# One of a product group's weight sums made in DRAM by the DMA, nine more such groups, and idle memory put to use

## The chip, the core and the metric

The kernel runs on one core of a Trainium2 chip. TensorE (PE) multiplies, VectorE (DVE) and ScalarE (ACT) do elementwise work, GpSimd (POOL) and SyncE (SP) here do little computing: SP issues the loads of the weights. The metric is the time of one execution in microseconds on the device; lower is better. Before the change the median of three runs is 1473.39 us (1472.85 to 1474.01).

## The reference

One decoder layer on 256 tokens of width 2048, in float32: a combined input projection, a state-space half and an attention half, an output projection, and an MLP with a squared ReLU.

```python
u = rmsnorm(h, norm_mix_pre)
z, xbc, dt, q, k, v = split(u @ w_in)              # 2048 -> 12320 columns
y_ssm = ssd(conv(xbc), dt) gated by z, grouped rmsnorm
y_att = mixture of three causal dilated windows over q, k, v (16 heads of 128)
h = h + rmsnorm(concat(y_ssm, y_att) @ w_out)      # 4096 -> 2048
ff = relu(rmsnorm(h) @ w_up)                       # 2048 -> 8192
h = h + rmsnorm((ff * ff) @ w_down)                # 8192 -> 2048
```

Nearly all the time is in four matrix products: by w_in, w_out, w_up and w_down.

## The kernel before

**A product in float32 precision.** TensorE's fast float32 type (fp32r) keeps fewer bits, so every operand is split into hi + lo: ScalarE rounds it into hi (L139), VectorE takes the remainder into lo (L140). A product is then three matmuls: hi by hi, hi by lo, lo by hi (`row_tile`, L256 to L264). Activations are split once and kept; weights come from DRAM as raw tiles, 256 rows of 512 columns (512 KB, two blocks of 128 rows: KB = 2), by SP (`fetch`, L144), are split into a pair of tiles from a ring of five (`parts`, BUFS = 5), and used once. There are four raw tiles (RAWS = 4). Where the memory of dead activations is free, `fetch_next` takes raw tiles from that too (`uc`, where "ua", "ub" and "uc" are parts of one activation).

**A seven-product group.** For one step k (two row blocks) a plain treatment of two neighbouring column blocks a and b, for both halves of the tokens, is 8 products, 24 matmuls. `seven` (L311) does it in 7 products, 21 matmuls, in the way of Strassen and Winograd: it needs sums of weight blocks (`e`, two of them, `t4`, and the sum of b's two blocks, in place in `raw_b`) and sums of activations (`sums_of_acts`, L293, made once per k and kept in idle memory). All weight sums are adds on VectorE (`add_in_line`, L223; the add itself is L225), and `e`, `raw_b` and `t4` are then split like weights. Seven products go to four extra PSUM banks (`more`) and three of the four result banks (`acc`); `combine_new` adds `more` up on VectorE into SBUF after the last group of a unit.

**A unit** (`unit`, L362) is one such pair of column blocks over all of K: for each k in a given order either a plain pair (two calls of `row_tiles`) or a group; then the last plain steps, first for block a, then for b, each with a function at its end (`at_end`) that takes the result out of PSUM. For w_up that function (`up_end`) adds the combined part, scales, squares, and puts a generator (`turned`) on a list (`waiting`); it later transposes the result on TensorE into the same PSUM bank (L1223) and splits it (sl or al on VectorE). `pump` runs one step of that list after each k and block; at the first group of a unit `drain` runs the rest. The next unit uses the old `acc` as its `more`, so its first group writes the banks that these transposes use.

**The stages** in order: projections for the state-space half and its scan (to about 372 us), queries, keys and two units for the values (V), w_out (two units), the first half of w_up's hidden columns (a block of features in another layout and three units), w_down over them (two units), the second half of w_up (four units) and of w_down (two). Groups per unit: V 4; w_out 3 and 6; up 3 each (`UP_SEVENS`); down 5, 5, 5, 6: 59 in all.

**What sets the order.** Engines run their own queues in order. A scheduler places instructions by priority and by data they need; weights' splits and sums have high priority and are kept in program order on ScalarE and VectorE (`in_line`). GpSimd's queue has pow for the norms (`rmix`, `rmlp`, `rff`) and, in the state-space half, small products. The tile "junk" has one buffer, the temporaries "r" two.

Of the kernel before, what the change touches and what calls it, by code (L numbers as in the profile page):

```python
# [39 lines left out]
KB = 2  # L40
MASKED = -1.0e30
# [10 lines left out]
UP_SEVENS = (2, 4, 5)  # L52
V_SEVENS = (1, 3, 5, 6)

# [20 lines left out]
def hymba_layer(ctx: ExitStack, tc: tile.TileContext, x, norm_mix_pre, w_in, conv_w, conv_b, dt_bias, a_log,  # L75
# [38 lines left out]
    cst = cp.tile([P, consts.shape[1]], F32, name="cst")  # L114
    ident = cst[:, 0:P]
    triu = cst[:, P:2 * P]
    two = cst[:, 2 * P:2 * P + 32]
    m0 = cst[:, 2 * P + 32:3 * P + 32]
    m1 = cst[:, 3 * P + 32:5 * P + 32]
# [24 lines left out]
    def fetch(src, k0, c0, step=KB, into=None):  # L144

        raw = wp.tile([P, KB, NB], F32, name="raw", bufs=RAWS) if into is None else into
        for j in range(0, KB, step):
            rs = slice((k0 + j) * P, (k0 + j + step) * P)
            nc.sync.dma_start(raw[:, j:j + step], src[rs, c0:c0 + NB].rearrange("(k p) n -> p k n", p=P))
        return raw  # L150


    def tmp():
        if "own" in room:
            room["own"].rotate(1)
            return room["own"][0]
        return hp.tile([P, NB], F32, name="r", bufs=2)
# [8 lines left out]
    def in_place_of_u():  # L166
        a, b = big.tile([P, SUMS, 2, S], F32R, name="ua"), big.tile([P, KB, 2, S], F32R, name="ub")
        room["sums"] = [a[:, k] for k in range(SUMS)] + [b[:, k] for k in range(KB)]
        room["raw"] = big.tile([P, NK - SUMS - KB, NB], F32, name="uc")
        room["turn"] = -RAWS  # L170
        room["acts"] = part
        sums_of.clear()

    def in_place_of_h(acts):

        a = hp.tile([P, 3 * KB, 2, S], F32R, name="ha")
        room["sums"] = [a[:, k] for k in range(3 * KB)]
        if acts is part:
            b = hp.tile([P, KB, 2, S], F32R, name="hb")
            room["sums"] += [b[:, k] for k in range(KB)]  # L180
            room["sums"] += [hp.tile([P, 2, S], F32R, name="wpost", bufs=2) for _ in range(2)]
        else:
            b = hp.tile([P, NT, NB], F32, name="hb")
            room["shared"] = [[b[:, t] for t in range(NT)],
                              [hp.tile([P, NB], F32, name="wpost", bufs=2) for _ in range(NT)]]
        room["raw"] = None
        room["acts"] = acts
        sums_of.clear()

    def fetch_next(src, k0, c0):  # L190

        if room["raw"] is None:
            return fetch(src, k0, c0)
        turn = room["turn"]
        room["turn"] += 1
        n = KB * (turn % (RAWS + (NK - SUMS) // KB - 1) - RAWS)
        return fetch(src, k0, c0, into=None if turn < 0 or n < 0 else room["raw"][:, n:n + KB])
# [3 lines left out]


# [20 lines left out]
    def add_in_line(dst, a, b):  # L223
        with in_line():
            line["dve"] = nc.vector.tensor_tensor(dst, a, b, op=ALU.add)  # L225
# [85 lines left out]
    def seven(src, ca, cb, k, acc, more, first, last):  # L311
# [4 lines left out]
        with tc.high_priority(offset=AHEAD):  # L316
            raw_a = fetch_next(src, k * KB, ca)
            raw_b = fetch_next(src, k * KB, cb)
            e, t4 = sum_tile(), tmp()
            add_in_line(e[:, 0], raw_a[:, 0], raw_b[:, 0])  # L320
            add_in_line(e[:, 1], e[:, 0], raw_b[:, 1])
# [3 lines left out]
            add_in_line(raw_b[:, 0], raw_b[:, 0], raw_b[:, 1])  # L325
# [33 lines left out]
    def order_of(ks, by_seven):  # L359
        return [(k, k in by_seven) for k in ks]  # L360

    def unit(src, n, order, last, acc, more, combine, lag=0, at_end=(None, None), first=True, ending=None):  # L362
# [17 lines left out]
        for b in range(2):  # L380
            if b and ending:
                ended.append(ending(cols[b], last, acc))
            else:
                row_tiles(src, cols[b], last, acc[b::2], room["acts"], False, True, lag if b else 0, at_end[b],
                          fetch=fetch if b else fetch_next)
# [41 lines left out]
    cw = cp.tile([P, 4, 32], F32, name="cw")  # L427
    bias_b = cp.tile([P, 32], F32, name="bias_b")
    a_b = cp.tile([P, 32], F32, name="a_b")
    skip_b = cp.tile([P, 32], F32, name="skip_b")  # L430
# [19 lines left out]
    def load_parameters():  # L450
# [4 lines left out]
        nc.sync.dma_start(cst[:, P:], consts[:, P:])  # L455
# [77 lines left out]
    with tc.high_priority(offset=2 * AHEAD), tc.manual_schedule():  # L533
        nc.sync.dma_start(cst[:, 0:P], consts[:, 0:P])
# [21 lines left out]
    rbq = cp.tile([P, S], F32, name="rbq")  # L556

    mid = ExitStack()
# [5 lines left out]
    dt = cp.tile([P, NT, 32], F32, name="dt")  # L564
    dA = cp.tile([P, NT, 32], F32, name="dA")
    acs = cp.tile([P, NT, 32], F32, name="acs")
    eacs = cp.tile([P, 32], F32, name="eacs")
    toend = cp.tile([P, 32], F32, name="toend")
# [240 lines left out]
    def in_place_of_last_heads():  # L809
# [3 lines left out]
        room["raw"], room["acts"] = None, act_u  # L813
# [5 lines left out]
    def two_values(vb):  # L819
# [16 lines left out]
        unit(w_in[:, COL_V:], vb, order_of(range(7), V_SEVENS), (7,), acc, more,  # L836
# [15 lines left out]
    waiting.append(in_place_of_last_heads())  # L852
    qk.append(keys_too(1))
# [36 lines left out]
    def in_mw(n):  # L890
        return [[mw[:, t, columns(n + b)] for t in range(NT)] for b in range(2)]

    def combine_onto(n, more):

        with tc.high_priority(offset=AHEAD):
# [4 lines left out]
            nc.vector.tensor_tensor(mw[:, 0, a], v, mw[:, 0, a], op=ALU.add)  # L900
            nc.vector.tensor_tensor(mw[:, 1, a], u, mw[:, 1, a], op=ALU.add)
            nc.vector.tensor_tensor(mw[:, 1, a], more[3], mw[:, 1, a], op=ALU.add)
            nc.vector.tensor_tensor(u, more[1], u, op=ALU.add)
            nc.vector.tensor_tensor(mw[:, 0, b], mw[:, 0, b], u, op=ALU.subtract)
            nc.vector.tensor_tensor(u, more[3], u, op=ALU.add)
            nc.vector.tensor_tensor(mw[:, 1, b], mw[:, 1, b], u, op=ALU.subtract)

    def mixed(n, t, acc):

        cs = columns(n)  # L910
        nc.vector.tensor_tensor(mw[:, t, cs], acc, mw[:, t, cs], op=ALU.subtract if n % 2 else ALU.add)
        junk = hp.tile([P, NB], F32, name="junk")
        nc.scalar.activation(junk, mw[:, t, cs], AF.Square, accum_out=ssq[:, t, n:n + 1])
        nc.vector.tensor_mul(mw[:, t, cs], mw[:, t, cs], wpost[n])

    def mix_to_up(c0, ks, acc):
# [22 lines left out]
        def mix(t, n):  # L939
            m = mw[:, t, columns(n)]  # L940
            nc.vector.tensor_tensor(m, acc[n - 2 + 2 * t], m, op=ALU.subtract if n % 2 else ALU.add)

        def mix_square(t, n):
            junk = hp.tile([P, NB], F32, name="junk")
            nc.scalar.activation(junk, mw[:, t, columns(n)], AF.Square, accum_out=ssq[:, t, n:n + 1])

        def weight(t, n):
            nc.vector.tensor_mul(mw[:, t, columns(n)] if n == 2 else weighed[:, t], mw[:, t, columns(n)], wpost[n])

        def add(t, n):  # L950
            cs = columns(n)
            nc.vector.scalar_tensor_tensor(of_h(t, cs), weighed[:, t] if n == 3 else mw[:, t, cs], rm[:, t:t + 1],
# [126 lines left out]
    early = 5  # L1079
    for k in range(early):  # L1080
# [16 lines left out]

    new_h()
    mw = hp.tile([P, NT, D], F32, name="mw")
# [18 lines left out]
    unit(w_out, 0, order_of(range(early, 14), (6, 9, 12)), (14, 15), acc, more,  # L1118
# [13 lines left out]
    def first_hidden(t, acc):  # L1132

        ts = slice(t * P, (t + 1) * P)
        r = hp.tile([P, NB], F32, name="r", bufs=2)
# [8 lines left out]
    unit(w_out, 2, order_of((0, 6, 1, 9, 2, 12, 3, 4, 5, 8, 7, 10), (6, 9, 12, 4, 8, 10)), (11, 13, 14, 15), acc, more,  # L1144
# [5 lines left out]
    def finish(t, acc):  # L1150


        with tc.high_priority(offset=(1 + t) * AHEAD):
# [3 lines left out]
            nc.vector.tensor_add(mw[:, t, cs], acc, mw[:, t, cs])  # L1157
            junk = hp.tile([P, NB], F32, name="junk")
            nc.vector.tensor_tensor_reduce(junk, mw[:, t, cs], mw[:, t, cs], 1.0 / D, some, ALU.mult, ALU.add, m)
            nc.gpsimd.tensor_tensor(rff[:, t:t + 1], m, half[:, 0:1], op=ALU.pow)  # L1160
            nc.vector.tensor_mul(mw[:, t, cs], mw[:, t, cs], wpost[3])
            if t:
# [5 lines left out]
                nc.tensor.matmul(p, dg, mw[:, t, columns(0)], start=False, stop=True)  # L1168
# [4 lines left out]
            for n, cs in enumerate(pieces if t else (columns(0), *pieces)):  # L1173
                nc.vector.scalar_tensor_tensor(of_h(t, cs), mw[:, t, cs], rff[:, t:t + 1], of_h(t, cs),
# [3 lines left out]
    def onto(n):  # L1178

        def at_end(t, acc):  # L1180
            m = mw[:, t, columns(n)]
# [12 lines left out]
    def out_of_place():  # L1194

        yield from copies(in_dram, of_h, 4)
        in_place_of_h(act_u)
# [31 lines left out]
    for b in range(2):  # L1229
        r = hp.tile([P, 2, S], F32, name="r", bufs=2)  # L1230
# [5 lines left out]
    for hf in range(2):  # L1236
        if hf:
            in_place_of_h(act_u)
# [56 lines left out]
```

## Time and profile before

| | before |
|---|---|
| median of three runs | 1473.39 us (1472.85 to 1474.01) |
| profiled execution: span from first to last instruction | 1471.1 us (its own time is not listed apart; the median lies 2.3 us above the span) |
| busy: TensorE, VectorE, ScalarE, GpSimd | 1461.2, 1239.6, 861.1, 47.8 us |
| DMA: moved, mean rate | 287.31 MB, 195 GB/s |
| DMA queue of SP, share of 16 engines | 58.9% |

Rows of the timeline give start, duration, engine, line, operation, output and inputs. A matmul's duration includes its way through the array; matmuls overlap, so their pace is the distance between starts. "PEld" is the weight load ahead of a matmul. VectorE's instructions overlap a little in the same way. A row of waits names the engine and line that waited, what released it, the total, the number and the longest. L lines are lines of the kernel before.

### The profile page before, as it was taken

The numbers are of one execution on the slowest core, as the hardware profiler recorded it, in microseconds if no ns is written. First come the engines' busy times: TensorE is split into PE (matmuls) and PEld (weight loads), VectorE is DVE, ScalarE is ACT, GpSimd is POOL, SyncE is SP. The second block draws the span as 40 slices with busy tenths as digits, with TensorE's granted clock in tenths as the row PEclk, the third lists the DMA queues.
The fourth block names the chain that finished last, engine by engine and source line by source line (L and its number), as shares of the span: only waits on it lengthen the run. The fifth ranks groups of instructions, "written<-read, shape, count | busy, mean of one in ns | idle before, by whom it ended". The sixth has DMA issues, their size and how long they took to land.

```text
span 1471.1 us, 20006 instructions
## 1 busy us (share of the span) xinstructions
PE 1461.2 (99%) x7216; PEld 1231.4 (84%) x7216; DVE 1239.6 (84%) x1849; ACT 861.1 (59%) x1188; POOL 47.8 (3%) x67
## 2 busy tenths in 40 slices
PE   9999999999999999999999999999999999999998
PEld 8888888888888888888888888888888888888886
DVE  6798797898497696588989989889887898989998
ACT  7475675465456565555557566655554666665553
POOL 0003100210000000000000000000000000000000
PEclk9999999999999999999999999999999999999999
DMA  7665566555657476566657566655665666576853
GB/s 272 208 205 182 179 184 194 174 172 167 177 168 207 122 208 192 191 229 210 204 177 237 165 194 201 210 175 191 213 223 174 201 201 205 172 235 202 273 200 114
DMA packets 151299, 287.31 MB, mean 195 GB/s; under 512 B 11696, under 2 KB 14624, under 8 KB 151200
## 3 DMA queue, kind: packets, MB, share of 16 engines
q1 hardware_dynamic: 143472, 272.50, 58.9%
q10 hardware_dynamic: 7728, 13.54, 2.8%
q8 instruction: 56, 0.92, 0.3%
q14 instruction: 43, 0.35, 0.1%
HBM read 281.78 MB, written 4.23 MB: 194 GB/s over the span
## 4 chain that ended last, share of the span: by engine, by line
PE 94%; DVE 3%; issue 1%; ACT 1%; DMA 1%; POOL 0%; POOLq 0%; SPq 0%; ACTq 0%; DVEq 0%
PE acc L393 17%; PE acc L262 12%; PE acc L263 12%; PE acc L264 12%; PE acc L396 9%; PE acc L345 4%; PE acc L346 4%; PE acc L344 4%; PE ps L263 3%; PE ps L262 3%; PE ps L264 3%; PE ps L346 2%; PE ps L344 2%; PE ps L345 2%; DVE lo L140 1%
## 5 line engine op out<-in xcount | busy, mean ns | idle before, releaser
L139 ACT ACTIVATE hi<-raw 128x1024 fp32r<-128x1024 f32 (+1 forms) x477 | 499.0, 1053 | 387.9 <-PE acc L393 111.9
L140 DVE TENSOR_TENSOR lo<-raw,hi 128x1024 fp32r<-128x1024 f32 (+1 forms) x477 | 579.9, 1220 | 135.7 <-ACT hi L139 127.9
L393 PE MATMUL acc<-ua,hi 128*128 128x512 f32 x680 | 186.3, 402 | 0.0
L393 PEld LDWEIGHTS acc<-ua,hi 128*128 128x128 f32 x680 | 119.7, 189 | 18.7
L262 PE MATMUL acc<-hi,ua 128*128 128x512 f32 x280 | 112.0, 400 | 0.0
L396 PEld LDWEIGHTS acc<-ua,lo 128*128 128x128 f32 x680 | 99.8, 189 | 11.6
L264 PE MATMUL acc<-hi,ua 128*128 128x512 f32 x280 | 109.3, 391 | 0.0
L263 PE MATMUL acc<-lo,ua 128*128 128x512 f32 x280 | 109.3, 390 | 0.0
L396 PE MATMUL acc<-ua,lo 128*128 128x256 f32 x680 | 102.9, 281 | 0.0
L262 PE MATMUL acc<-hi,sh 128*128 128x512 f32 x224 | 88.7, 397 | 0.0
L264 PE MATMUL acc<-hi,sl 128*128 128x512 f32 x224 | 87.3, 390 | 0.0
L263 PE MATMUL acc<-lo,sh 128*128 128x512 f32 x224 | 87.3, 390 | 0.0
L139 ACT ACTIVATE hi<-e 128x1024 fp32r<-128x1024 f32 x51 | 54.1, 1062 | 55.5 <-DVE e L225 50.3
L393 PE MATMUL acc<-uc,hi 128*128 128x512 f32 x272 | 77.6, 398 | 0.0
L263 PE MATMUL acc<-lo,ah 128*128 128x512 f32 x168 | 65.5, 390 | 0.4 <-DVE lo L140 0.4
L264 PE MATMUL acc<-hi,al 128*128 128x512 f32 x168 | 65.4, 389 | 0.0
L262 PE MATMUL acc<-hi,ah 128*128 128x512 f32 x168 | 65.4, 389 | 0.0
L264 PEld LDWEIGHTS acc<-hi,ua 128*128 128x128 f32 x280 | 52.6, 188 | 11.6
L140 DVE TENSOR_TENSOR lo<-e,hi 128x1024 fp32r<-128x1024 f32 x51 | 62.0, 1216 | 0.0
L262 PEld LDWEIGHTS acc<-hi,ua 128*128 128x128 f32 x280 | 52.6, 188 | 10.4 <-ACT ua L141 0.3
L263 PEld LDWEIGHTS acc<-lo,ua 128*128 128x128 f32 x280 | 52.7, 188 | 10.0
L264 PE MATMUL acc<-hi,uc 128*128 128x512 f32 x144 | 56.0, 389 | 0.0
(475 smaller groups left out, 3060.9 us busy)
## 6 DMA issues: line engine op xcount, KB each, us to landing
raw<-in_w_in_dram SPq DMA_DIRECT2D x189, 512.0 KB, 3.6
raw<-in_w_up_dram SPq DMA_DIRECT2D x128, 512.0 KB, 3.9
raw<-in_w_down_dram SPq DMA_DIRECT2D x110, 512.0 KB, 4.7
raw<-in_w_out_dram SPq DMA_DIRECT2D x46, 512.0 KB, 4.2
uc<-in_w_out_dram SPq DMA_DIRECT2D x18, 512.0 KB, 4.5
uc<-in_w_down_dram SPq DMA_DIRECT2D x18, 512.0 KB, 5.1
bc<-acs_d ACTq DMA_DIRECT2D x8, 512.0 KB, 4.5
xs<-in_x_dram SPq DMA_DIRECT2D x8, 256.0 KB, 6.3
```

Source lines behind the costliest of these rows:

```text
L139: return (nc.scalar.activation(hi, src, AF.Copy), nc.vector.tensor_tensor(lo, src, hi.bitcast(F32), op=ALU.subtract))
L140: nc.vector.tensor_tensor(lo, src, hi.bitcast(F32), op=ALU.subtract))
L262: nc.tensor.matmul(dst, a_h[:, r, ts], hi[:, j], start=begin and j == 0, stop=False)
L263: nc.tensor.matmul(dst, a_h[:, r, ts], lo[:, j], start=False, stop=False)
L264: product[t] = nc.tensor.matmul(dst, a_l[:, r, ts], hi[:, j], start=False, stop=end and j == KB - 1)
L344: nc.tensor.matmul(dst, a_h, hi[:, j], start=own and first, stop=False)
L345: nc.tensor.matmul(dst, a_h, lo[:, j], start=False, stop=False)
L346: nc.tensor.matmul(dst, a_l, hi[:, j], start=False, stop=own and last)
L393: nc.tensor.matmul(acc[f], hi[:, j, f * P:(f + 1) * P], u(k0 + j), start=k0 + j == 0, stop=False, skip_group_check=True)
L396: nc.tensor.matmul(acc[f][:, 0], lo[:, j, f * P:(f + 1) * P], u(k0 + j)[:, 0], start=False, stop=k0 + j == NK - 1, skip_group_check=True)
```

## The change

A group's sum of b's two row blocks is no longer made on VectorE. GpSimd's queue issues, four groups ahead, a copy of the first block of b (128 rows of 512 columns, 256 KB) from the weight in DRAM into one of five places in DRAM, and then a second transfer that adds the second block onto it (`accum_op`). SP then loads the sum and the second block into `raw_b` as two transfers of 256 KB in place of one of 512 KB. VectorE makes e[1] from a's first block and the sum, and e[0] by taking the second block of b off again.

An up unit has groups at k = 1, 3, 4 and 6 (before 2, 4 and 5), with 7 as the only last step (before 6 and 7); the second down unit and the third get a sixth group, in new orders. That is 7 + 1 + 1 = 9 more, 68 in all.

Memory: during the first half of up the buffer `mw` (now two tiles) serves as four more raw tiles, during the second half "ha" as three, during the first down half part of `mw` as two; in the second down unit `mw` holds two more sums. The up units' sums of activations lie in the upper half of the attention's activations `ah` and `al` instead of "ha". The temporaries "r" get four buffers. Constants and small parameters that only the first half needs move to a pool ("fp") that is given up with it. In the up units the loads keep their program order on SP.

On VectorE, one group in an up unit, before (L225 is an add, L140 the remainder of a split):

```order
L225 TENSOR_TENSOR e<-raw 128x512
L225 TENSOR_TENSOR e<-e,raw 128x512
L140 TENSOR_TENSOR lo<-raw,hi 128x1024
L225 TENSOR_TENSOR r<-e,raw 128x512
L225 TENSOR_TENSOR raw<-raw 128x512
L140 TENSOR_TENSOR lo<-e,hi 128x1024
```

And in the changed kernel (L246 and L144 are the same two lines; mw_6166 is a piece of `mw` used as a raw tile):

```order
L246 TENSOR_TENSOR e<-mw_6166 128x512
L246 TENSOR_TENSOR e<-e,mw_6166 128x512
L144 TENSOR_TENSOR lo<-mw_6166,hi 128x1024
L246 TENSOR_TENSOR r<-e,mw_6166 128x512
L144 TENSOR_TENSOR lo<-e,hi 128x1024
```

One add is gone; nothing else moved within the group.

On TensorE, the last set of transposes of an up unit's results before the next unit's first group; before the change it stands between two plain steps (twelve products follow it, then the group):

```order
L263 MATMUL ps<-lo,ua 128x512
L264 MATMUL ps<-hi,ua 128x512
L1223 MATMUL acc<-cst,r 128x128 x4
L262 MATMUL acc<-hi,ua 128x512
L263 MATMUL acc<-lo,ua 128x512
```

After it (L1305 are the transposes, L403 to L405 the group's products):

```order
L1305 MATMUL acc<-ident,junk 128x128
L1305 MATMUL acc<-ident,r 128x128
L1305 MATMUL acc<-ident,junk 128x128
L1305 MATMUL acc<-ident,r 128x128 x2
L1305 MATMUL acc<-ident,junk 128x128
L1305 MATMUL acc<-ident,r 128x128
L403 MATMUL acc<-hi,ua 128x512
L404 MATMUL acc<-lo,ua 128x512
L405 MATMUL acc<-hi,ua 128x512
```

Three of four sets, interleaved, now stand directly ahead of the group; this is so at five of the seven unit ends, all but the two ahead of a down unit.

On GpSimd's queue, around the norm between w_out and w_up, before:

```order
L134 TENSOR_TENSOR gr<-rm,half 128x2
L723 TENSOR_TENSOR xs<-xs,yo 128x256
L134 TENSOR_TENSOR gr<-rm,half 128x2
L885 TENSOR_TENSOR rmix<-mean,half 128x1 x2
L885 TENSOR_TENSOR rmlp<-mean,half 128x1 x2
```

And after (L270 copies a block into a place in DRAM, L271 adds the other onto it):

```order
L270 DMA pair_89<-in_w_up_dram 128x512
L271 DMA pair_89<-in_w_up_dram 128x512
L270 DMA pair_90<-in_w_up_dram 128x512
L271 DMA pair_90<-in_w_up_dram 128x512
L956 TENSOR_TENSOR rmix<-mean,half 128x1 x2
L956 TENSOR_TENSOR rmlp<-mean,half 128x1 x2
L270 DMA pair_91<-in_w_up_dram 128x512
```

The transfers of five up groups now stand ahead of `rmix` in that queue.

The core of the diff:

```diff
-UP_SEVENS = (2, 4, 5)
+UP_SEVENS = (1, 3, 4, 6)
+PAIRS_AHEAD = 4
...
+        if pair is not None:
+            nc.sync.dma_start(raw[:, 0], pair)
+            loaded[:] = [nc.sync.dma_start(raw[:, 1], src[(k0 + 1) * P:(k0 + 2) * P, c0:c0 + NB])]
+            return raw
...
-        return hp.tile([P, NB], F32, name="r", bufs=2)
+        return hp.tile([P, NB], F32, name="r", bufs=4)
...
+    def beside_up(raws, turn):
+
+        room["sums"] = [v[:, k:k + KB] for k in range(NK // 2, NK, KB) for v in (ah, al)]
+        b = hp.tile([P, NT, NB], F32, name="hb")
+        room["shared"] = [[b[:, t] for t in range(NT)],
+                          [hp.tile([P, NB], F32, name="wpost", bufs=2) for _ in range(NT)]]
+        room["raw"], room["turn"], room["acts"], room["chain"] = raws, turn, act_u, True
+        sums_of.clear()
...
+        n = turn % (RAWS + len(room["raw"])) - RAWS
+        into = None if turn < 0 or n < 0 else room["raw"][n]
+        with ExitStack() as order:
+            for last in loaded if room.get("chain") else ():
+                order.enter_context(tc.issue_after(last.ins))
+            return fetch(src, k0, c0, into=into, pair=pair)
...
+    def next_pair():
+
+        if not pairs:
+            return
+        src, ca, k = pairs.pop(0)
+        cb = slice(ca + NB, ca + 2 * NB)
+        d = places[len(paired) % len(places)]
+        if len(paired) < len(places):
+            nc.gpsimd.dma_start(d[:, 0:1], sh[:, NK - 1, 0:1].bitcast(F32))
+        nc.gpsimd.dma_start(d, src[k * KB * P:(k * KB + 1) * P, cb])
+        nc.gpsimd.dma_start(d, src[(k * KB + 1) * P:(k * KB + 2) * P, cb], accum_op=ALU.add)
+        paired.append((src, ca, k, d))
+
+    paired = []
+    places = [dram.tile([P, NB], F32, name=f"pair{i}") for i in range(PAIRS_AHEAD + 1)]
...
             raw_a = fetch_next(src, k * KB, ca)
-            raw_b = fetch_next(src, k * KB, cb)
+            raw_b = fetch_next(src, k * KB, cb, pair_of(src, ca, k))
             e, t4 = sum_tile(), tmp()
-            add_in_line(e[:, 0], raw_a[:, 0], raw_b[:, 0])
-            add_in_line(e[:, 1], e[:, 0], raw_b[:, 1])
+            add_in_line(e[:, 1], raw_a[:, 0], raw_b[:, 0])
+            add_in_line(e[:, 0], e[:, 1], raw_b[:, 1], ALU.subtract)
             hl_a = parts()
             split_in_line(*hl_a, raw_a)
             add_in_line(t4, e[:, 1], raw_a[:, 1])
-            add_in_line(raw_b[:, 0], raw_b[:, 0], raw_b[:, 1])
...
+            plan(("up", hf), w_ups[hf], n, range(7), UP_SEVENS)
+        if hf == 0:
+            plan(("down", 0), w_down, 0, range(14), (4, 6, 9, 11, 13))
+            plan(("down", 0), w_down, 2, (0, 4, 1, 6, 2, 9, 3, 11, 5, 13, 7, 10, 8), (4, 6, 9, 11, 13, 10))
+    plan(("down", 1), w_downs[1], 0, (0, 1, 2, 3, 4, 6, 5, 8, 7, 9, 10, 11, 12, 13), (3, 6, 8, 9, 11, 13))
...
+    with tc.high_priority(offset=AHEAD):
+        for _ in range(PAIRS_AHEAD):
+            next_pair()
...
-            unit(w_up[:, hf * 4096:], fb, order_of(range(6), UP_SEVENS), (6, 7), acc, more,
+            unit(w_ups[hf], fb, orders[("up", hf), fb], (7,), acc, more,
```

192 lines of the change are left out of this document (111 added, 81 removed).

## Prediction

> **What bounds the kernel now.** I read the page first (engine shares, slices, the chain), then what TensorE waited for.
>
> ```profile
> PE 1461.2 (99%) x7216; PEld 1231.4 (84%) x7216; DVE 1239.6 (84%) x1849; ACT 861.1 (59%) x1188; POOL 47.8 (3%) x67
> DVE  6798797898497696588989989889887898989998
> PEclk9999999999999999999999999999999999999999
> PE 94%; DVE 3%; issue 1%; ACT 1%; DMA 1%; POOL 0%; POOLq 0%; SPq 0%; ACTq 0%; DVEq 0%
> ...
> PE ps L1168 <- ACT dg L1167: 2.3, 1, 2.3
> ...
> PE acc L263 <- DVE lo L140: 0.4, 1, 0.4
> PE acc L345 <- DVE lo L140: 0.3, 1, 0.3
> ```
>
> The chain is 94% TensorE at full granted clock, and its waits for other engines are one at the very end (2.3 us) and tenths elsewhere. A busy TensorE need not be at its peak, so I took its pace from the timeline, over one seven-product group and its surroundings in an up unit:
>
> ```profile
> 917.31 0.60 PE L1223 MATMUL acc<-cst,r 128*128 128x128 f32 x4
> 917.66 0.49 PE L262 MATMUL acc<-hi,ua 128*128 128x512 f32 x1
> ...
> 920.52 0.39 PE L344 MATMUL ps<-hi,ua 128*128 128x512 f32 x1
> ...
> 925.28 0.39 PE L262 MATMUL acc<-hi,ua 128*128 128x512 f32 x1
> ```
>
> From 920.52 to 925.28 lie the 21 products of a seven-product group: 4.76 us, 0.2267 us each, back to back. A plain pair of blocks is 24 such products, 5.44 us. Each matmul taken out is worth 0.2267 us as long as its neighbours stay fed. So the question is whether VectorE, the loads and the new transfers keep up.
>
> VectorE by stage (columns: stretch, length, then busy time and count of PE, PEld, DVE, ACT, POOL, then clock, DMA share, GB/s); the rows are a values unit, the first hidden block, an up unit, a down unit:
>
> ```profile
> 388.00:440.00 52.00, 51.73 (x251) 43.33 (x250) 39.40 (x47) 25.82 (x31) 0.00 (x0) 1.00 0.56 163
> 783.00:823.00 40.00, 40.00 (x219) 34.10 (x218) 37.17 (x68) 27.21 (x49) 1.08 (x2) 1.00 0.72 226
> 1164.00:1207.00 43.00, 43.00 (x198) 35.55 (x197) 38.40 (x47) 28.68 (x36) 0.00 (x0) 1.00 0.65 200
> 1295.00:1378.00 83.00, 83.00 (x374) 68.65 (x373) 77.94 (x102) 47.21 (x55) 0.00 (x0) 1.00 0.67 217
> ```
>
> VectorE is busy 38.4 of 43.0 us in an up unit and 77.9 of 83.0 in a down unit: near the bound, not on it.
>
> **The change, part by part.**
>
> *Nine more groups.* Each saves 24 - 21 = 3 products; the listing of the changed kernel has 27 matmuls of 512 columns fewer. 27 x 0.2267 = **-6.1 us** on TensorE, which is the path.
>
> *One sum moved off VectorE.* The cost of a group's VectorE work, from the timeline of one group:
>
> ```profile
> 1179.07 0.68 DVE L225 TENSOR_TENSOR e<-raw 128x512 f32<-128x512 f32 x1
> 1179.79 0.69 DVE L225 TENSOR_TENSOR e<-e,raw 128x512 f32<-128x512 f32 x1
> 1180.40 1.22 DVE L140 TENSOR_TENSOR lo<-raw,hi 128x1024 fp32r<-128x1024 f32 x1
> 1181.53 0.68 DVE L225 TENSOR_TENSOR r<-e,raw 128x512 f32<-128x512 f32 x1
> 1182.14 0.68 DVE L225 TENSOR_TENSOR raw<-raw 128x512 f32<-128x512 f32 x1
> 1182.74 1.22 DVE L140 TENSOR_TENSOR lo<-e,hi 128x1024 fp32r<-128x1024 f32 x1
> ```
>
> By starts, an add of 512 columns takes 0.60 (0.72 where the next one reads it) and a split of 1024 takes 1.13. The removed add is the 1182.14 row. All 59 old groups save 0.60: 35.4 us. A new group adds, over a plain pair, three adds (0.72 + 0.61 + 0.61), the split of e (1.13) and of t4 (0.60): 3.67, nine times 33.0. Three more sums of activations (L293) are five operations of at most 0.60: up to 3.0 each. VectorE is as busy as before in all, but not by stage: an up unit goes from 38.4 to 38.4 - 3 x 0.60 + 3.67 = 40.3 us, in 43.0 - 0.7 = 42.3. It stays under TensorE with 2 us to spare; a down unit with five groups falls by 3.0. Cost on the path 0.
>
> What a group has in hand is the tightest point. In the second of two consecutive groups:
>
> ```profile
> 1189.50 1.22 DVE L140 TENSOR_TENSOR lo<-e,hi 128x1024 fp32r<-128x1024 f32 x1
> ...
> 1191.82 0.39 PE L345 MATMUL acc<-lo,ha 128*128 128x512 f32 x1
> ```
>
> The split of e ends at 1190.72 and is first read at 1191.82: 1.1 us early. In the change its position on VectorE comes one add sooner, so the lead grows to 1.7, and the two short waits on L140 quoted above (0.4 and 0.3) should mostly go: bounds -0.7 and 0, taken **-0.5**, since 0.6 is nearly all of either.
>
> *The first group comes one pair sooner.* The order (1,3,4,6) puts an up unit's first group after one plain pair, not two, and the transposes of the last unit's results, formerly after every twelve products, pile up: one set of four, then three sets straight ahead of the group, at five of the seven unit ends. These write the very banks that the group's own sums need. Before:
>
> ```profile
> 919.37 0.68 DVE L140 TENSOR_TENSOR al<-acc,ah 128x512 fp32r<-128x512 f32 x1
> ```
>
> The last set starts at 917.31 and its bank is free at 919.37 + 0.68 = 920.05: 2.74 us, and 0.47 before the group. In the change three sets take 3 x 0.35 = 1.05 us (0.35 is 917.31 to 917.66) right before the group, so by the same 2.74 the first bank is free 1.69 after the group's start, the others 0.60 later each: 2.29 and 2.89. The listing has ten products ahead of the first that writes one of these banks: 2.27, then 2.95 and 3.63. It just holds. If one weight split stands ahead on VectorE (1.13) it is 0.55 late, with two 1.7. Bounds 0 and 1.7 at each of five ends; near the lower one, since the banks' order fits: 0.2 each, **+1.0**.
>
> *The pair transfers.* 68 groups get a copy and an accumulating transfer on the POOL queue, 256 KB each, and the 512 KB load of the second tile becomes two of 256 KB on SP. Nothing in the trace moves DRAM to DRAM or accumulates. The nearest rows are the 256 KB moves of h to and from DRAM:
>
> ```profile
> q1 hardware_dynamic: 143472, 272.50, 58.9%
> ...
> h_d<-ha ACTq DMA_DIRECT2D x6, 256.0 KB, 4.3
> ha<-h_d ACTq DMA_DIRECT2D x6, 256.0 KB, 6.9
> ```
>
> Two in series are 8.6 to 13.8 us. A pair is issued four groups ahead, some 43 us in an up unit (42.7 / 4 = 10.7 between groups), so latency is covered; pace is what could fail. POOL issues the next copy without waiting for the last accumulation, so the pace is nearer one transfer than two: 4.3 to 6.9, under 10.7. Cost 0; without that cover (13.8 against 10.7) 3.1 for each of 28 up groups, 87 us. The Trainium skill ("DMA: Bandwidth & Descriptors", Anatomy of one DMA — SWDGE (gpsimd) path) gives such a DMA about 2.0 us plus its bytes at 436 GB/s: as an estimate 2.6 us for 256 KB, 5.2 in series, by which even the serial pace is safe; no run here shows it.
>
> *First pairs, POOL and SP queues.*
>
> ```profile
> 354.48 0.48 DVE L142 SCALAR_TENSOR_TENSOR sl<-ps,par,sh 128x256 fp32r<-128x256 f32 x1
> ...
> L225 DVE TENSOR_TENSOR cT<-raw x8: 682/684/693, 397.9 to 530.5; 128x512 f32<-128x512 f32 x8
> ...
> POOL rmix L885 <- DVE mean L884: 437.9, 2, 431.8
> ...
> SPq L149 <- DVE lo L140: 24.1, 13, 3.8
> ```
>
> The first pairs wait for the last sh (354.5 + 0.5) and are read from 397.9: 43 us for at most 13.8. Behind POOL's waits stands only rmix, which had been idle for 431.8 us; the last pair ahead of it needs a load of the out unit's last group, long past. Uncovered it would be one 6.9 once. SP waits 24.1 us in an up unit for raw tiles to come free, so 68 more issues cost nothing.
>
> *Load on the 16 DMA engines.* 0.589 x 16 x 1471.1 / 143472 = 0.097 us for a packet of about 2 KB, so a pair's 256 packets take 1.55 us of all engines. An up unit's four raise the share from 0.65 by 6.2 / 42.7 = 0.15. In the up and the first down units raw tiles get idle memory besides the four; in the values units not. A load there may land up to 1.55 late, against 0.60 gained: 0 to 0.95 for each of eight groups, taken **+0.3** in all, since not every load meets a pair. The fourth sum of activations falls into the hidden block, where VectorE has 40.0 - 37.2 = 2.8 us and needs up to 3.0: **+0.2**. Two more "r" buffers and the moved constants cost and save nothing: no wait above names them.
>
> Sum: -6.1 - 0.5 + 1.0 + 0.3 + 0.2 = -5.1. The profiled execution's span is 1471.1, 2.3 below the median of the three runs, 1473.39; I take those 2.3 as lying outside the span and unchanged. 1471.1 - 5.1 + 2.3 = **1468.3 us**.
>
> **The rivals.**
>
> *The unit ends eat it.* At 1.2 us for each of five ends, 1.0 becomes 6.0: 1473.3, no change (at the upper bound, 1.7, it is 8.5: 1475.8). For it speak the interleaved sets and that junk has one buffer, so its second result waits for the first set; against it the 0.47 us and ten products of cover.
>
> *The pairs set the pace (slower).* SP issues in order, so a late pair holds every load behind it. It decides once a pair takes over 10.9 us in an up unit (28 x 0.2 eats the gain). At 12 it is 28 x 1.3 = 36: 1505; at 13.8, 1555. For it: an accumulation reads its target too, and the upper row is 6.9. Against: two transfers overlap, and POOL has no other work in these stages. The Trainium skill ("SBUF — State Buffer", SBUF: two separate sides) has a rule against this change: GpSimd can't write a DMA's descriptors while VectorE runs in a mode that uses both ports, which would slow every pair. The same page says tensor_tensor has no such mode, and that is nearly all of VectorE's work here; no run here shows it.
>
> *Loads come late (slower).* Where there are four raw tiles only (eight values groups, six in the second down unit), 0.95 each: 13 us, 1481. Decides above 0.5 us each. For it: DMA share 0.65 and more; against: leads grow.
>
> *The change does less than it says.* Ruled out for the products, which are counted; if VectorE's add weren't the tight step, -0.5 becomes 0: 1468.8.
>
> **How the numbers follow.** About 3 us (0.2%) is what a measurement of this kernel can tell from no change. Forecast, with its small variants, 0.61 (1466 to 1470.4); unit ends 0.16, no change; late loads 0.09 and pair pace 0.14, slower: 0.61, 0.16, 0.23. The low end is all of 6.1 and 0.7 with nothing lost, and a little: 1466. The high end takes in late loads, 1481; the pair pace is left out. The forecast's own range is 1466 to 1470.4.
>
> **What would show it.** Right: TensorE's products still 0.227 apart; about 1455 us busy; the L140 waits gone; at an up unit's first group no wait on sl or al above 0.3; raw tiles of a pair landing within the 4.3 to 6.9 us above and SP's waits still on VectorE, not on a pair. Wrong: PE waiting for the split of acc at unit ends; SP waiting on the pool's transfers; an accumulation over 6.9 us; ScalarE waiting on raw in the values units.

## The result and the profile after

The changed kernel takes 1468.24 us in the median of five runs (1466.73 to 1470.74), beside 1473.39 for the kernel before (five runs, 1472.85 to 1474.01). The ratio is 0.9966, with an interval of 0.9956 to 0.9976: 5.2 us faster, where 1468.3 was forecast. The profiled execution has a span of 1466.5 us, 4.6 less than before; its own time is 1468.24, so 1.7 us lie outside the span.

The head of the page of the changed kernel (busy time, share of the span and instructions of each engine; DMA queues with packets, megabytes and share of the 16 engines; the chain by engine):

```profile
PE 1454.9 (99%) x7189; PEld 1226.0 (84%) x7189; DVE 1240.3 (85%) x1850; ACT 877.4 (60%) x1209; POOL 143.6 (10%) x208
...
q1 hardware_dynamic: 144560, 272.50, 58.9%
q0 software_dynamic: 15392, 35.66, 12.1%
...
PE 86%; DVE 7%; DMA 3%; issue 2%; ACT 1%; POOL 0%; SPq 0%; POOLq 0%; ACTq 0%; DVEq 0%
```

TensorE has 27 matmuls fewer and 6.3 us less to do; VectorE has as much as before (1239.6), now for 68 groups instead of 59. A queue q0 is new: the transfers that make the sums. The chain still runs on TensorE, but 10% of it now lies on VectorE and DMA, 4% before: these have less to spare.

VectorE by stage, in the stretches of the changed kernel that answer to the four shown of before (values unit, hidden block, up unit, down unit; same columns):

```profile
388.00:440.00 52.00, 52.00 (x254) 43.90 (x253) 39.05 (x46) 27.42 (x32) 5.44 (x8) 1.00 0.76 209
783.00:823.00 40.00, 40.00 (x218) 34.05 (x217) 37.61 (x73) 27.19 (x50) 2.50 (x4) 1.00 0.73 228
1157.00:1200.00 43.00, 42.60 (x196) 35.13 (x196) 40.84 (x51) 30.13 (x37) 6.27 (x9) 1.00 0.89 260
1286.00:1370.00 84.00, 84.00 (x379) 69.32 (x378) 79.92 (x108) 52.42 (x63) 8.17 (x12) 1.00 0.84 256
```

An up unit has VectorE busy for 40.84 us of 43 (38.40 before), and the DMA engines for 0.89 of the time (0.65 before).

What TensorE waited for in the changed kernel (total, number, longest; us):

```profile
PE ps L1250 <- ACT dg L1249: 2.3, 1, 2.3
...
PE ps L838 <- DVE mx L845: 0.9, 1, 0.9
PE acc L323 <- DVE lo L144: 0.7, 2, 0.5
PE acc L1305 <- ACT junk L1294: 0.4, 1, 0.4
```

The 2.3 at the very end is the old one, and the two rows left out stand alike in the kernel before. The other three shown are new and take the place of the two short waits on L140. The first place of the two waits on L144 and the one on L1305, from the timeline (the second down unit of the first half, then the end of an up unit):

```profile
1087.29 0.50 PE L323 MATMUL acc<-lo,sh 128*128 128x512 f32 x1 [0.49 <-DVE lo L144]
...
1166.03 0.27 PE L1305 MATMUL ps<-ident,r 128*128 128x128 f32 x1
1166.71 0.33 PE L1305 MATMUL acc<-ident,junk 128*128 128x128 f32 x1 [0.40 <-ACT junk L1294]
```

The transfers, from the list of DMA issues of the changed kernel (number, size, median us from issue to landing):

```profile
raw<-in_w_in_dram SPq DMA_DIRECT2D x181, 512.0 KB, 4.1
raw<-in_w_down_dram SPq DMA_DIRECT2D x79, 512.0 KB, 5.2
raw<-in_w_up_dram SPq DMA_DIRECT2D x65, 512.0 KB, 4.9
...
pair<-in_w_up_dram POOLq DMA_DIRECT2D x56, 256.0 KB, 5.4
raw<-pair SPq DMA_DIRECT2D x50, 256.0 KB, 4.5
pair<-in_w_down_dram POOLq DMA_DIRECT2D x46, 256.0 KB, 6.0
```

Loads of raw tiles land later than before, which had 3.6 (w_in), 4.7 (w_down) and 3.9 (w_up).

### The profile page after: what moved, and what is told of

Same layout as the page of the kernel before. It is cut to its first block, busy times and chain, and to the rows that moved or that the text cites. A ratio compares the mean times of both kernels' runs of the same rounds, so it can differ in the third digit from the quotient of the medians.

```text
span 1466.5 us, 20371 instructions
## 1 busy us (share of the span) xinstructions
PE 1454.9 (99%) x7189; PEld 1226.0 (84%) x7189; DVE 1240.3 (85%) x1850; ACT 877.4 (60%) x1209; POOL 143.6 (10%) x208
## 3 DMA queue, kind: packets, MB, share of 16 engines
q1 hardware_dynamic: 144560, 272.50, 58.9%
q0 software_dynamic: 15392, 35.66, 12.1%
## 4 chain that ended last, share of the span: by engine, by line
PE 86%; DVE 7%; DMA 3%; issue 2%; ACT 1%; POOL 0%; SPq 0%; POOLq 0%; ACTq 0%; DVEq 0%
PE acc L462 17%; PE acc L323 10%; PE acc L324 10%; PE acc L322 10%; PE acc L465 9%; PE acc L404 4%; PE acc L405 4%; PE acc L403 4%; DVE lo L144 4%; PE ps L324 2%; PE ps L323 2%; PE ps L322 2%; PE ps L405 2%; PE ps L404 2%; PE ps L403 2%
## 5 line engine op out<-in xcount | busy, mean ns | idle before, releaser
L143 ACT ACTIVATE hi<-raw 128x1024 fp32r<-128x1024 f32 (+1 forms) x418 | 437.2, 1051 | 298.2 <-PE acc L462 105.1
L144 DVE TENSOR_TENSOR lo<-raw,hi 128x1024 fp32r<-128x1024 f32 (+1 forms) x418 | 509.0, 1222 | 108.7 <-ACT hi L143 105.0
L143 ACT ACTIVATE hi<-e 128x1024 fp32r<-128x1024 f32 x60 | 63.8, 1063 | 78.3 <-DVE e L246 70.6
L322 PE MATMUL acc<-hi,ua 128*128 128x512 f32 x236 | 93.7, 397 | 0.0
L323 PE MATMUL acc<-lo,ua 128*128 128x512 f32 x236 | 92.1, 390 | 0.0
L324 PE MATMUL acc<-hi,ua 128*128 128x512 f32 x236 | 92.1, 390 | 0.0
L144 DVE TENSOR_TENSOR lo<-e,hi 128x1024 fp32r<-128x1024 f32 x60 | 73.1, 1219 | 0.0
L324 PE MATMUL acc<-hi,al 128*128 128x512 f32 x156 | 60.7, 389 | 0.0
L322 PE MATMUL acc<-hi,ah 128*128 128x512 f32 x156 | 60.7, 389 | 0.0
L323 PE MATMUL acc<-lo,ah 128*128 128x512 f32 x156 | 60.7, 389 | 0.0
L404 PE MATMUL acc<-lo,ah 128*128 128x512 f32 x151 | 58.8, 389 | 0.0
L403 PE MATMUL acc<-hi,ah 128*128 128x512 f32 x151 | 58.8, 389 | 0.0
L405 PE MATMUL acc<-hi,al 128*128 128x512 f32 x151 | 58.8, 389 | 0.0
L144 DVE TENSOR_TENSOR lo<-uc,hi 128x1024 fp32r<-128x1024 f32 x38 | 46.2, 1222 | 13.0 <-ACT hi L143 12.8
```

Source lines behind the costliest of these rows:

```text
L143: return (nc.scalar.activation(hi, src, AF.Copy), nc.vector.tensor_tensor(lo, src, hi.bitcast(F32), op=ALU.subtract))
L144: nc.vector.tensor_tensor(lo, src, hi.bitcast(F32), op=ALU.subtract))
L322: nc.tensor.matmul(dst, a_h[:, r, ts], hi[:, j], start=begin and j == 0, stop=False)
L323: nc.tensor.matmul(dst, a_h[:, r, ts], lo[:, j], start=False, stop=False)
L324: product[t] = nc.tensor.matmul(dst, a_l[:, r, ts], hi[:, j], start=False, stop=end and j == KB - 1)
L403: nc.tensor.matmul(dst, a_h, hi[:, j], start=own and first, stop=False)
```

## The experiments

All of them start from the changed kernel; a diff shows what was edited in it. Ratios are against runs of the kernel before that were taken along with them (medians 1473.29 to 1473.54 us). None of them leaves out any of the computation.

**The two main parts, each without the other.** Three kernels fill a square of two parts: the sums made by transfers, and the nine groups. In one the sum is made on VectorE again and the 59 old groups are back, so that only the memory and the buffers are changed:

```diff
-            raw_b = fetch_next(src, k * KB, cb, pair_of(src, ca, k))
+            raw_b = fetch_next(src, k * KB, cb)
...
+            add_in_line(raw_b[:, 0], raw_b[:, 0], raw_b[:, 1])
...
-UP_SEVENS = (1, 3, 4, 6)
+UP_SEVENS = (2, 4, 5)
```

> Only the memory, buffer and load-order part of the change: the sum stays on VectorE and the 59 groups stay as before. Theory (the gain is the nine groups' products): within 1.5 us of the kernel before, 1472 to 1475, TensorE busy 1461. Rival (idle memory for raw tiles is worth something by itself): 1471 or less, with ScalarE's waits for raw tiles in the up units gone.

Measured: 1473.2 us, ratio 0.9998 [0.9989, 1.0007]. ScalarE's waits for w_up's raw tiles, 23.9 us in all in the kernel before, are gone from its list, and the time is the same. In the second the transfers stay and only the 59 groups and their orders are put back (the last two lines of that diff, and the old orders of two down units):

> Sum made in DRAM and the memory part, but the 59 groups in the old places. Theory: 1473.4 less the two short waits on the split (0.5) and plus a few tenths for crowded loads: 1472 to 1474. VectorE some 35 us less busy, and that buys nothing. Rival 1 (the transfers cost something by crowding): over 1475. Rival 2 (VectorE's relief is the gain): under 1470.

Measured: 1474.34 us, 1.0008 [0.9999, 1.0017]. VectorE is busy for 1206.5 us, 33 less than before, and that alone buys nothing. TensorE's two short waits for splits are gone too, but 2.2 us at L838 (a wait for the attention's maximum) have come in. In the third the 68 groups stay, and the sum goes back to VectorE (the first lines of the diff alone):

> The 68 groups and the memory part, but the sum on VectorE and no pair transfers. Theory: an up unit needs 38.4 + 4.27 = 42.7 us of VectorE in 42.3 to 42.7 of TensorE, so VectorE's lead runs out there: 0.4 to 2 us for each of seven units, 1471 to 1482, with waits of TensorE on the split in the up units. Rival (the buffers hide it, the DRAM sum isn't needed): 1468, same as the change.

Measured: 1474.68 us, 1.0007 [0.9999, 1.0016]. Its up unit, and what the weight loads of TensorE waited for:

```profile
1157.00:1200.00 43.00, 42.34 (x191) 33.99 (x190) 42.33 (x53) 29.30 (x38) 0.00 (x0) 1.00 0.66 196
```

```profile
PEld acc L404 <- ACT hi L143: 3.7, 4, 1.1
PEld acc L405 <- DVE lo L144: 3.5, 10, 0.8
```

One of these waits, from the timeline (line numbers of the groups are one higher here):

```profile
1184.10 0.68 DVE L246 TENSOR_TENSOR ha<-ha 128x512 f32<-128x512 f32 x1
...
1184.95 1.06 ACT L143 ACTIVATE hi<-ha 128x1024 fp32r<-128x1024 f32 x1 [1.33 <-DVE ha L246]
...
1186.06 0.50 PE L404 MATMUL acc<-hi,ah 128*128 128x512 f32 x1 [0.65 <-ACT hi L143]
```

VectorE is busy for 42.33 of 43.00 us, and TensorE now waits for splits inside the groups (L404, L405). In the rows shown it waits for ScalarE's rounding of b's tile (here in "ha"), and ScalarE for the very add that the change moves away. So the products saved are worth nothing while the sum stays on VectorE, and the sum moved away is worth nothing while the products stay: neither part alone is told from no change, both together give 5.2 us. VectorE, at 38.4 of 43.0 before, had no room for a fourth group of the old kind.

**Four ahead or one.** The transfers of a pair issued one group ahead of its use:

```diff
-PAIRS_AHEAD = 4
+PAIRS_AHEAD = 1
```

> Pairs made one group ahead, two places in DRAM. A pair takes about 10 to 11 us from copy to landed sum, consecutive groups are 4.8 us apart, others 10.2 to 15.6. Theory (the four groups are the cover): SP waits for pairs at each second of two consecutive groups and partly elsewhere, up to 5 us for some 20 groups, less what raw tiles in hand cover: 1470 to 1560. Rival (raw tiles in hand are cover enough): 1468 to 1469.

Measured: 1467.71 us, 0.9959 [0.9947, 0.9972], not told from the changed kernel. Pairs are late now, and it is SP that shows it:

```profile
SPq L157 <- DVE lo L144: 473.7, 238, 9.8
...
SPq L152 <- DMA pair<-in_w_up_dram: 56.0, 11, 10.1
```

SP stands for up to 10.1 us at a pair that isn't done, and none of TensorE's waits comes of it: the raw tiles that are already loaded bridge it. The distance of four groups was not what kept the pairs harmless.

**More transfers.** Each pair's copy is made twice, so three transfers per sum:

```diff
+        for _ in range(2):
-        nc.gpsimd.dma_start(d, src[k * KB * P:(k * KB + 1) * P, cb])
+            nc.gpsimd.dma_start(d, src[k * KB * P:(k * KB + 1) * P, cb])
```

> Each pair's copy made twice, so three transfers in series on POOL's queue instead of two, 68 x 256 KB more moved. By the change's trace the wait of POOL for a copy is 4 to 5 us, so three in series with the last overlapped take about 10 to 12 us, against 10.7 between groups in an up unit. Theory (four groups ahead cover latency, pace decides from about 10.9): from no change to 28 x 1.3 = 36 us slower, 1468 to 1505, and SP waits for a pair if over 1475. Rival (the load of the DMA engines decides, whose share was 0.84 to 0.89 in the up and down units): over 1505.

Measured: 1477.34 us, 1.0024 [1.0013, 1.0036], some 9 us over the changed kernel, with runs from 1470.3 to 1481.0. SP waits for no pair, though the expectation had it wait from 1475 us on. TensorE waits for splits in several places (line numbers are one higher here; the last row is the queue of the transfers):

```profile
PE acc L324 <- DVE lo L144: 1.6, 2, 0.9
PE ps L324 <- DVE lo L144: 1.5, 2, 0.8
PE ps L323 <- ACT hi L143: 1.1, 2, 0.9
...
q0 software_dynamic: 20832, 53.49, 15.6%
```

So it is not the pace of the pairs that gives way first. Extra traffic costs time without a pair being late. That it does so by making raw tiles late fits the waits for splits, and the median landing of w_down's tiles, which went from 5.2 to 5.6 us; it was not measured apart.

**Without the idle memory for raw tiles.** The up units and the first down units have their four raw tiles only; the sums and everything else stay:

```diff
-        beside_up([*(v for m in mws for v in tiles_of(m, (0, NB)))], -2 * RAWS)
+        beside_up([], 0)
...
-            beside_up([*(a[:, k:k + KB] for k in range(0, 3 * KB, KB))], 0)
+            beside_up([], 0)
...
-        room["raw"], room["turn"], room["acts"] = [*tiles_of(mws[1], (0, NB))], 0, part
+        room["raw"], room["turn"], room["acts"] = [], 0, part
```

> The change without the idle memory as raw tiles in the up units and the first down unit: four raw tiles there, everything else kept. Theory (idle tiles are what covers loads that land 1 to 2 us later beside the pair transfers): ScalarE waits for raw tiles in the up units and TensorE for splits, 1470 to 1476. Rival (four tiles would do, as they did before): 1468, the same as the change.

Measured: 1484.68 us, 1.0071 [1.0057, 1.0085]: 16 us over the changed kernel, far above either expectation. TensorE's longest entry, then ScalarE and TensorE at one unit end:

```profile
PE acc L1305 <- ACT junk L1294: 10.6, 8, 2.1
```

```profile
905.15 1.06 ACT L143 ACTIVATE hi<-raw 128x1024 fp32r<-128x1024 f32 x1 [0.56 <-DMA raw<-in_w_up_dram]
911.33 1.06 ACT L143 ACTIVATE hi<-raw 128x1024 fp32r<-128x1024 f32 x1 [5.11 <-DMA raw<-in_w_up_dram]
912.30 0.71 ACT L1293 ACTIVATE junk<-junk,rmlp 128x512 f32<-128x512 f32 x1
...
918.97 0.62 ACT L1294 ACTIVATE junk<-junk 128x512 f32<-128x512 f32 x1
...
919.64 0.33 PE L1305 MATMUL acc<-ident,junk 128*128 128x128 f32 x1 [2.12 <-ACT junk L1294]
```

ScalarE stands for 5.11 us at a split whose raw tile hasn't landed. SP had issued that load at 903.2, and it took 8.0 us, beside 4.7 in the median of w_up's raw tiles in this kernel; a pair's second transfer, issued at 901.9, was under way beside it for 8.5. Behind ScalarE's wait queue the scaling and squaring of the unit's results (junk), and TensorE's transposes of them come 2.12 us late. Most of the loss thus does not reach TensorE as a missing weight but through the unit's end.

**The same with the first group later.** If the loss needed the new place of the first group, moving the group from k = 1 to k = 2 should undo most of it. With the spare raw tiles kept, that move alone:

```diff
-UP_SEVENS = (1, 3, 4, 6)
+UP_SEVENS = (2, 3, 4, 6)
```

> The change with up groups at 2, 3, 4, 6 instead of 1, 3, 4, 6: the first group again after two plain pairs, the transposes spread as before, but three groups in a row. Theory (the piled-up transposes cost only some tenths, and a row of three groups takes 2 us of lead each from about 7): within 1.5 us of the change, 1467 to 1470. Rival (the unit ends are where the missing microsecond of the gain went): 1466 to 1467; rival 2 (the lead runs out in the third group): 1471 or more.

Measured: 1469.75 us, 0.9971 [0.9959, 0.9983], not told from the changed kernel. And without the spare tiles as well (both diffs):

> The changed kernel without idle raw tiles in the up and the first down units (as in the run that took 1484.68), and with an up unit's first group at k = 2, so that six products of plain work lie between the last transposes and the group. Theory, the loss sits at the unit ends (a raw tile comes late, ScalarE in its order makes junk late, the transposes and then the group wait): TensorE's waits on junk fall from 10.6 us to under 3, and the time to 1472 to 1478. Rival, loads are late all over the up units: TensorE waits for as long, on splits, and the time stays at 1482 or more.

Measured: 1490.33 us, 1.0108 [1.0095, 1.0121]. The theory fell, and the rival has the time right but not the place:

```profile
PE acc L1305 <- ACT junk L1294: 11.4, 11, 1.8
PE ps L1305 <- ACT junk L1294: 3.2, 3, 1.2
```

TensorE waits for the unit's results even more (14.6 us in all), now ahead of the transposes in the middle of plain products. Room between transposes and group is no help, since the transposes themselves are late. The kernel with the group at k = 1 had shown it already: half of its 10.6 us (0.56, 1.83, 1.46 and 1.43) stood at the two unit ends ahead of a down unit, where no group follows the transposes.

**The same with the old groups.** The sums by transfers, no spare raw tiles, and 59 groups:

> The sums by transfers, the old 59 groups and orders, and no idle raw tiles in the up and the first down units (buffers else as changed). Theory, the transfers that run beside the loads make these late and so make the spare raw tiles necessary: slower than the 1474.34 of the same kernel with them, by 3 us or more. Rival, the nine new groups and their places make them necessary: within 1.5 us of 1474.34, as the kernel before has no such tiles either and doesn't wait.

Measured: 1477.65 us, 1.0025 [1.0014, 1.0036], with runs from 1474.92 to 1480.36; with the spare tiles it was 1474.34, 1.0008. The theory's 3 us are there. But its profile puts most of that elsewhere:

```profile
PE ps L838 <- DVE mx L845: 2.9, 1, 2.9
...
PE acc L1305 <- ACT junk L1294: 0.7, 1, 0.7
```

Only 0.7 us stand at a unit end. The 2.9 at L838 is a wait in the attention ahead of the output projection, which this edit doesn't touch, and which differs between kernels anyway: 0.9 in the changed kernel, 2.2 with spare tiles and 59 groups, 3.0 with the first group later. So what the tiles are worth with the old groups is not settled beyond "much less than 16 us". It is with the nine groups on top of the transfers that they are needed; no run has the nine groups without transfers and without the tiles.

**Two temporaries instead of four.**

```diff
-        return hp.tile([P, NB], F32, name="r", bufs=4)
+        return hp.tile([P, NB], F32, name="r", bufs=2)
```

and likewise at the two other places that make an "r".

> The changed kernel with two temporaries r as before, not four. Theory, they cost and save nothing: 1467.2 to 1469.2. Rival, transposes at the unit ends, which now come in three sets together and each read an r, need them: 1470 to 1474, with waits ahead of L1305.

Measured: 1474.32 us, 1.0011 [1.0001, 1.0021]; the whole gain is gone. VectorE ahead of an up unit's first group in this kernel, and the product that reads the split of e:

```profile
1166.17 0.69 DVE L1292 TENSOR_TENSOR junk<-acc,wpost 128x512 f32<-128x512 f32 x1 [0.36 <-PE ps L1305]
1168.43 0.69 DVE L144 TENSOR_TENSOR sl<-ps,sh 128x512 fp32r<-128x512 f32 x1 [1.56 <-ACT sh L143]
1170.10 0.69 DVE L246 TENSOR_TENSOR r<-e,ha 128x512 f32<-128x512 f32 x1 [0.98 <-PE acc L1305]
1170.73 1.29 DVE L144 TENSOR_TENSOR sl<-acc,sh 128x512 fp32r<-128x512 f32 x2
1171.94 0.68 DVE L144 TENSOR_TENSOR sl<-ps,sh 128x512 fp32r<-128x512 f32 x1
1172.53 1.22 DVE L144 TENSOR_TENSOR lo<-e,hi 128x1024 fp32r<-128x1024 f32 x1
...
1173.81 0.50 PE L404 MATMUL acc<-lo,ah 128*128 128x512 f32 x1
```

The group's third weight sum (t4) is an "r" too, and so are the unit's results until they are transposed. With two buffers the sum waits for the transposes (L1305) to be done, at 1170.10, while TensorE starts the group at 1170.04; behind it, in program order, stand the splits of the results and of the group's e, which ends at 1173.75, just ahead of the product at 1173.81. Measured by the distance between starts, TensorE loses about 1 us at each of the five unit ends; the list of waits names none of it, as products that don't need the split still run in between, more widely spaced. The span is 4.9 us longer than the changed kernel's. With four, by the timeline of the changed kernel, the same sum is made ahead of the transposes:

```profile
1163.46 0.69 DVE L246 TENSOR_TENSOR r<-e,ha 128x512 f32<-128x512 f32 x1
1164.07 0.69 DVE L1292 TENSOR_TENSOR junk<-acc,wpost 128x512 f32<-128x512 f32 x1
1164.67 1.22 DVE L144 TENSOR_TENSOR lo<-e,hi 128x1024 fp32r<-128x1024 f32 x1
```

There the group starts at 1167.77 and its e is split by 1165.89. The rival's time came true, but the wait is the sum's on the transposes, not the transposes' on an r.

**Two more groups.** In the first out unit, with four pairs ahead:

```diff
-    plan("out", w_out, 0, range(EARLY, 14), (6, 9, 12))
+    plan("out", w_out, 0, (5, 6, 7, 8, 11, 9, 13, 10, 12), (6, 8, 9, 10, 12))
```

> The change with two more groups in the first out unit (6, 8, 9, 10, 12 in place of 6, 9, 12), where VectorE is idle a third of the time. Theory: 6 products fewer, 6 x 0.2267 = 1.4 us less than the change, 1466.9. Rival (the pair transfers or the sums of activations arrive late there): 1468 or more.

Measured: 1469.07 us, 0.9972 [0.9960, 0.9983]. With one pair ahead:

> The changed kernel with pairs issued one group ahead and two more groups in the first out unit. By products 6 x 0.2267 = 1.4 us under the 1467.71 of one group ahead: 1466.4. Rival: a wait for a split in the out unit takes it again, as in the run with two more out groups: 1467.7 or a little more.

Measured: 1469.73 us, 0.9971 [0.9960, 0.9982]. Neither is told from the changed kernel. Both have the same entry among TensorE's waits; the row is of the first:

```profile
PE acc L403 <- ACT hi L143: 1.0, 1, 1.0
```

One wait for a split takes most of the 1.4 us of six products. No version tried is measurably better than the change itself.

## Why the prediction was right

- **Nine groups, -6.1:** held. Busy time of TensorE fell by 6.3 us.
- **The two waits on L140, -0.5:** they went, but others came. Measured by the distance between starts, beyond a matmul's own 0.23, the two old ones were 0.42 (436.76 to 437.41) and 0.57 (1439.62 to 1440.42); in their place stand 0.65 (1086.41 to 1087.29) and 0.33 (1389.38 to 1389.94). Net 0, where -0.5 was taken.
- **Five unit ends, +1.0:** the reckoning of the banks held, closely. At the end whose group starts at 1167.77 the second and third bank are free 2.81 and 3.41 us later (2.29 and 2.89 were forecast) and written at 3.10 and 3.78; no wait of TensorE names sl or al. One end costs 0.56, by another wait: a transpose there waits for ScalarE's squared result (junk), which no term of the sum priced. The 11 to 15 us of the kernels without spare tiles are waits of this second kind. They show how sensitive the unit ends are to a late ScalarE, and nothing about the banks.
- **Late loads in the values units, +0.3:** mechanism right, size off. One load is late:

```profile
ACT hi L143 <- DMA raw<-in_w_in_dram: 5.0, 3, 4.1
```

  This is ScalarE's wait from 425 to 455 us in the changed kernel; in the kernel before the longest there is 1.6. Some 9 us after that load the attention's maximum (mx) comes late, and TensorE stands for 1.17 at 452.2. In the kernels without transfers this stall isn't there; in those with them it has anything from nothing (one group ahead, and two more groups in the out unit) to 3.0 us. That this load is what delays mx was not tried.
- **The fourth sum in the hidden block, +0.2:** no wait of TensorE on it is seen. VectorE was busy for 37.61 of 40 us there, 37.17 before.
- **Sum.** -6.1 - 0.42 - 0.57 + 0.65 + 0.33 + 0.56 + 1.17 = -4.4; the spans differ by -4.6, the medians by -5.2. The last step, "those 2.3 as lying outside the span and unchanged", misread a number: in all later runs of the kernel before, 1.7 to 1.85 us lie outside the span, as in the changed kernel. The profiled execution of before was thus about 0.5 us faster than the median, and the medians differ by that much more than the spans. That the total met the forecast to 0.1 us is luck in part: late loads were 0.9 too low and the L140 term 0.5 too good; unit ends (0.4), the hidden block (0.2) and the forecast by the spans (0.5) were too high, and 0.2 is not accounted for.
- **The pair transfers, 0:** the cost held: SP waits for no pair. The bracket of 4.3 to 6.9 us holds in the median only. The copies (L270) land after 2.9 to 9.7 us, median 5.2, and the accumulating transfers (L271) after 4.2 to 9.4, median 6.6; the 5.4 and 6.0 above mix the two. So one sign of being wrong, an accumulation over 6.9 us, did show, and it cost nothing. One after the other the two would take 5.2 + 6.6 = 11.8 us, over the 10.7 between groups; but they overlap, as the prediction had it: the next copy is issued 1.30 us after an accumulation (1166.56 and 1167.86 below), long before that can have landed. The other reason given, latency covered by four groups' distance, isn't needed: one group does as well. The estimate of 2.6 us from the Trainium skill ("DMA: Bandwidth & Descriptors", Anatomy of one DMA — SWDGE (gpsimd) path) is half of what a copy takes here. Of the slowing that the Trainium skill ("SBUF — State Buffer", SBUF: two separate sides) describes for descriptors the trace shows no sign, though no run tests it: between a sum's copy and its second transfer POOL waits 337.0 us in 67 waits for the copy to land, 5.0 each and so no longer than a copy takes to land, with VectorE busy beside it. POOL's timeline in an up unit of the changed kernel:

```profile
1162.49 0.55 POOL L270 DMA_DIRECT2D pair<-in_w_up_dram  x1 [2.25 <-DMA raw<-pair]
1166.56 0.81 POOL L271 DMA_DIRECT2D pair<-in_w_up_dram  x1 [3.51 <-DMA pair<-in_w_up_dram]
1167.86 0.55 POOL L270 DMA_DIRECT2D pair<-in_w_up_dram  x1 [0.49 <-DMA ha<-pair]
1173.35 0.82 POOL L271 DMA_DIRECT2D pair<-in_w_up_dram  x1 [4.94 <-DMA pair<-in_w_up_dram]
```

- **Load on the engines:** undersized. By q0's share, 0.121 x 16 x 1466.5 / 68 = 41.8 us of one engine, or 2.6 us of all sixteen, for a pair, where 1.55 was taken. In an up unit that is 4 x 2.6 / 42.7 = 0.24 of share, and the share rose by 0.24, not 0.15. The prediction priced an accumulating packet like that of a load; the run with each copy made twice says that this is where it fell short (last section).
- **"Two more r buffers cost and save nothing: no wait above names them":** this step failed, by about 6 us. The trace of before names no such wait, and with the old groups four buffers buy nothing (1473.2 us with the memory and buffers alone). With the nine groups and the first one's new place they are a condition of the gain.
- **Idle memory:** named only as cover for a load up to 1.55 us late. Without it the kernel loses 16 us. The "late loads" rival (1481, decides above 0.5 us a load) comes near this case in cause and time, but put it where there are four tiles anyway; there it cost 1.2 at most.
- **VectorE near the bound:** held. An up unit was to need 40.3 us and has 40.84 in 43. With 68 groups and the sum on VectorE, its 42.33 of 43.00 us eat the whole gain.

## What to carry to other kernels

A change that takes work off the bounding engine can need several parts that are each worth nothing: here the saved products pay only if VectorE is relieved, and then only with spare raw tiles and four temporaries. So cost a buffer count in the new order of the work, not by the waits of the old one: ask which tiles will be held by whom when the moved instruction comes. And trace a late load along the in-order engine that first touches it; it surfaces where the queue behind it has the least slack, here 5 us of ScalarE became 2 us of TensorE at transposes that need no weights.

## What the hardware showed unexpectedly

- An accumulating transfer takes over twice the engine time of a plain one. With each copy made twice, 17.83 MB more (53.49 against 35.66), the queue's time went from 0.121 x 16 x 1466.5 = 2839 to 0.156 x 16 x 1476.6 = 3686 us of one engine. By this estimate, which takes a copy to cost the same in both kernels, a copy inside DRAM costs 847 / 17.83 = 47.5 us a MB, about as much as a load with 0.589 x 16 x 1466.5 / 272.50 = 51. What is left for the accumulating transfers is (2839 - 847) / 17.83 = 112 us a MB.
- Loads slow down from two sides. Their landing in w_up went from 3.9 to 4.9 us (into the spare tiles 5.4 and 6.6); with the memory alone changed, and no transfers, it is 4.4 already, presumably because more loads are under way at once.
- A queue that issues in order can stand for 10 us at a time without any cost on the bounding engine: with one group ahead SP did, for 56.0 us in 11 waits, and the time was 1467.71 us.
